# Attention heads scored and turned in groups on the tensor engine, in a two-layer streaming encoder

## The chip, the cores and the metric

The kernel runs on one core of a Trainium2 chip. Five engines of the core work side by side, each through its own list of instructions: TensorE (PE in the profile, with PEld for its loads of the stationary operand), VectorE (DVE), ScalarE (ACT), GpSimd (POOL) and SyncE (SP), which here only issues transfers. The metric is the device time of one execution in microseconds (us), lower is better.

## The reference

The input x is 256 tokens of 1024 numbers, in float32. Each of two layers is a SwiGLU feed-forward, a token mixing and a second feed-forward, each between two RMS norms:

```python
f = swiglu(rmsnorm(x, ffn1_pre_g[l]), ffn1_w_gate[l], ffn1_w_up[l], ffn1_w_down[l])
x = x + FFN_RESIDUAL_WEIGHT * rmsnorm(f, ffn1_post_g[l])
m = token_mixing(rmsnorm(x, mix_pre_g[l]), w_in[l], rel_bias[l], ..., w_out[l], lambda_init)
x = x + rmsnorm(m, mix_post_g[l])
f = swiglu(rmsnorm(x, ffn2_pre_g[l]), ffn2_w_gate[l], ffn2_w_up[l], ffn2_w_down[l])
x = x + FFN_RESIDUAL_WEIGHT * rmsnorm(f, ffn2_post_g[l])
```

The mixing projects x by w_in to queries, keys and values of 16 heads of 64 columns in three groups, and multiplies what they return by w_out:

- A, 6 heads: softmax attention over chunks of 64 tokens with a learned bias by distance.
- B, 4 heads: differential attention. A head has two softmax maps of 32 query and key columns each; the weights are `p[:, :, 0] - lam * p[:, :, 1]`, and the output goes through an RMS norm.
- C, 6 heads: stick-breaking attention, `a = jnp.where(strict, jnp.exp(log_beta + suffix), 0.0)` with a suffix sum of log-sigmoids.

## The kernel before

**The large products.** Tokens, weights and products are float32. A weight piece of mostly 512 KB comes by a transfer that SP issues, into one of four raw buffers. `Stream.ahead` splits it in two parts: ACT casts the high part (L142), DVE subtracts it for the low part (L143). A product of tokens and weights is then three matmuls (L376 to L378). These are called the main matmuls below.

**The mixing.** `mix` first computes the values. Then come 16 columns of queries and keys, `pp_0` to `pp_15`: 24 main matmuls each, of 128x256, into one PSUM bank. ACT copies each finished column to `qkT` (L842 or L844). Group B uses columns 0 to 3 (its heads 0 and 1 the columns 0 and 1, its heads 2 and 3 the columns 2 and 3), C columns 4 to 9, A columns 10 to 15. After these comes the product with w_out (`down`, main matmuls of 128x512 into `acc` banks).

**What sets the order.** The attention runs in the gaps of the main matmuls. `slot(n)` is called after every 6 main matmuls of the columns (so four times in a column; column f has slots 4f to 4f+3) and, from slot 64 on, after every 3 matmuls of the product with w_out. Each head or pair is a generator whose steps have due times in the table `PLAN`. All events are sorted by due time, and slot n issues those due before n+1. The program order on each engine follows from that; a consumer waits where its operand or its buffer is not ready. The pieces of splitting (`stream.ahead`) are also events, at n+0.9.

**The steps.** `head_b` has nine: scores of map 0, its softmax, scores of map 1, its softmax, `combine` (the difference of the maps, DVE), `turned` (three transposes on TensorE into a bank pT), `turned_copy` (ACT), the output, its scale. `pair_c` takes two heads: scores of each head in a step of its own, three passes of ACT, splitting, the suffix sums on TensorE (u1, u0), subtraction, the exponential, both outputs, the copy. `head_a` has scores, `soft`, the normalisation, `turned`, `turned_copy`, the output, and for odd heads the copy of the pair's output. In `soft`, DVE adds the bias and takes the row minimum (L723), and ACT takes the exponential (L725), in two blocks of 128 and 256 columns.

**Rows and columns of the array.** The scores of one B map contract over 32 partitions, at 64*(h%2)+32*m; those of an A or C head over 64, at 64*(h%2). The outputs of A and C heads go to 64 of the 128 output partitions (`columns_out`). The transposes and B's outputs use the full array.

**Banks.** PSUM has two tags of four banks each, `acc` and `rot`, and each tag hands out its banks in turn. `where(kind)` takes a kind's tag from the ranges in `PLAN["acc"]`. The columns pp are `rot`; the scores of B and C are `acc`; those of A are `acc` while the due time is below the end of the range `sA`.

Of the kernel before, what the change touches and what calls it, by code (L numbers as in the profile page):

```python
# [9 lines left out]
F32 = mybir.dt.float32  # L10
# [3 lines left out]
ALU = mybir.AluOpType  # L14
AX = mybir.AxisListType

P = 128
SEQ = 256
# [6 lines left out]
NH_A, NH_B, NH_C = 6, 4, 6  # L25
# [3 lines left out]
YA, YB, YC = 0, 384, 640  # L29
# [9 lines left out]
PLAN = {  # L39
    "qk": [  # L40
        7.05, 7.1, 14.05, 16.05, 19.05, 23.05, 27.05, 33.05, 35.05, 39.05, 43.05, 47.05, 53.05, 55.05,
        59.05, 63.05
    ],
# [5 lines left out]
    ],  # L49
# [4 lines left out]
    ],  # L54
    "a": [
        [49.1, 49.25, 51.05, 54.05, 57.05, 61.05],
        [50.05, 58.1, 58.92, 66.1, 68.1, 69.05, 72.05],
        [58.25, 58.3, 58.4, 62.05, 62.1, 67.05],
        [57.15, 58.35, 58.94, 63.1, 65.05, 69.1, 69.25],
        [68.05, 69.15, 70.05, 74.05, 76.05, 78.05],  # L60
        [65.1, 66.05, 66.25, 71.05, 71.1, 81.05, 83.05],
    ],
    "sub": [
        55.1, 64.05
# [11 lines left out]
    "gain": 81.1,  # L76
    "table": 82.05,
    "tail": 5,
    "acc": {"pT": [14, 26], "oB": [-10, 40], "oC": [-36, -14], "sA": [-140, 52]},
}  # L80
NSPLIT = 9

# [82 lines left out]
def trunk_kernel(  # L165
# [7 lines left out]
    nc = tc.nc  # L173
# [7 lines left out]
    small = ctx.enter_context(tc.tile_pool(name="small", bufs=3))  # L181
    psum = ctx.enter_context(tc.tile_pool(name="psum", bufs=4, space=bass.MemoryType.PSUM))
# [118 lines left out]
    def split_copy(hi, lo, src):  # L301
        nc.scalar.copy(hi, src)
        nc.vector.tensor_sub(lo, src, hi.bitcast(F32))
# [274 lines left out]
    def mix(i, l, turn1):  # L578
        lam_init = 0.8 - 0.6 * math.exp(-0.3 * l)
        v = act.tile([P, 2, D], F32, tag="bigl2", name=f"v{l}")  # L580
# [25 lines left out]
        c = stream.used  # L606
# [24 lines left out]
        qkT = act.tile([P, 16, SEQ], F32, tag="bigh1", name=f"qkT{l}")  # L631
# [3 lines left out]
        biasA = yb[:, 512:2048].rearrange("p (h s) -> p h s", h=NH_A)  # L635
# [81 lines left out]
        def soft(nm, s, bias, tag):  # L717


            p = work.tile([P, 512], F32, tag=tag, bufs=TA if tag == "ta" else 3, name=f"p_{nm}")[:, :384]  # L720
            st = small.tile([P, 4], F32, tag="st" + tag, name=f"st_{nm}")
            for t, (a, b) in enumerate(((0, P), (P, 384))):
                nc.vector.tensor_tensor_reduce(p[:, a:b], s[:, a:b], bias[:, SEQ - (b - a) : SEQ], 1.0, 3e38,  # L723
                                               ALU.add, ALU.min, accum_out=st[:, t : t + 1])
                nc.scalar.activation(p[:, a:b], p[:, a:b], AF.Exp, bias=st[:, t : t + 1], scale=-1.0,  # L725
                                     accum_out=st[:, 2 + t : 3 + t])
            return p, st

        def turned(nm, p):
            pT = psum.tile([P, 3, P], F32, tag=where("pT"), name=f"pT_{nm}")  # L730
            for j in range(3):
                nc.tensor.transpose(pT[:, j, :], p[:, j * P : j * P + P], ident)
            return pT

        def turned_copy(nm, pT):
            w = work.tile([P, 4, P], F32, tag="tc", bufs=3, name=f"wT_{nm}")[:, :3, :]
            nc.scalar.copy(w, pT)
            return w

        def columns_out(o, half, vh, w0, w1):  # L740
            oh = o[64 * half : 64 * half + 64, :]
            nc.tensor.matmul(oh, lhsT=vh[:, 0, :], rhs=w0, start=True, stop=False)
            nc.tensor.matmul(oh[:, P:], lhsT=vh[:, 1, :], rhs=w1, start=False, stop=True)

        def scores(nm, q, k, tag):
            s = psum.tile([P, 384], F32, tag=tag, name=f"s_{nm}")
            nc.tensor.matmul(s[:, 0:P], lhsT=q[:, 0:P], rhs=k[:, 0:P], start=True, stop=True)
            nc.tensor.matmul(s[:, P:384], lhsT=q[:, P:SEQ], rhs=k, start=True, stop=True)
            return s
# [35 lines left out]
        def subnorm():  # L785
            yb4 = yB.rearrange("p t (h d) -> p t h d", h=NH_B)
            sq = work.tile([P, 2, NH_B, 64], F32, tag="ta", bufs=TA, name=f"sq{l}")
            nc.vector.tensor_mul(sq, yb4, yb4)
            ss = small.tile([P, 2, NH_B], F32, tag="ssb", bufs=1, name=f"ssb{l}")
            nc.vector.tensor_reduce(ss, sq, AX.X, ALU.add)  # L790
            nc.vector.tensor_scalar(ss, ss, 1.0 / 64, EPS, ALU.mult, ALU.add)
            r = rstd_of(ss.rearrange("p t h -> p (t h)"), 2 * NH_B, f"sub{l}")
            yield
            for t in range(2):
                yv, sv = yb4[:, t], sq[:, t]
                rv = r[:, t * NH_B : (t + 1) * NH_B].unsqueeze(2).broadcast_to([P, NH_B, 64])
                nc.vector.tensor_mul(sv, yv, rv)
                nc.vector.tensor_mul(yv, sv, gsub.unsqueeze(1).broadcast_to([P, NH_B, 64]))
            yield

        pair_out = {}

        def head_a(h):

            nm = f"a{l}_{h}"
            fq, fk, b = 10 + 2 * (h // 2), 11 + 2 * (h // 2), 64 * (h % 2)
            s = scores(nm, qkT[b : b + 64, fq, :], qkT[b : b + 64, fk, :], where("sA"))
            yield
            p, st = soft(nm, s, biasA[:, h, :], "ta")
            yield  # L810
            ri = small.tile([P, 2], F32, tag="ri", bufs=6, name=f"ria{l}_{h}")
            nc.vector.reciprocal(ri, st[:, 2:4])
            for t, (a, c) in enumerate(((0, P), (P, 384))):
                nc.vector.tensor_scalar(p[:, a:c], p[:, a:c], ri[:, t : t + 1], None, ALU.mult)
            yield
            pT = turned(nm, p)
            yield
            w = turned_copy(nm, pT)
            yield
            if h % 2 == 0:  # L820
                pair_out[h // 2] = psum.tile([P, SEQ], F32, tag="rot", name=f"o_{nm}")
            vs = slice(YA + 64 * h, YA + 64 * h + 64)
            columns_out(pair_out[h // 2], h % 2, v[:, :, vs], w[:, 0:2, :], w[:, 2, :])
            yield
            if h % 2:
                keep_y(h // 2, pair_out[h // 2])
                yield

        def keep_y(k, src):
            split_copy(xT[:, k, 0], xT[:, k, 1], src.rearrange("p (t c) -> p t c", t=2))  # L830
# [17 lines left out]
        def where(kind):  # L848
            a, b = PLAN["acc"][kind]
            return "acc" if a <= now[0] < b else "rot"  # L850

        def at(x, do):
            events.append((x, len(events), do))

        def steps(slots, gen):
            for x in slots:
                at(x, lambda: next(gen))
# [4 lines left out]
            steps(PLAN["b"][h], head_b(h))  # L862
        for j in range(NH_C // 2):
            steps(PLAN["c"][j], pair_c(j))
        for h in range(NH_A):
            steps(PLAN["a"][h], head_a(h))
        steps(PLAN["sub"], subnorm())
        for k in range(2):
            steps(PLAN["turn"][k], turn_b(k))
# [60 lines left out]
    for i in range(3 * DEPTH):  # L930
        turn1 = mix(i, i // 3, turn1) if i % 3 == 1 else ffn(i, turn1)
# [36 lines left out]
```

## Time and profile before

| | |
|---|---|
| times of the runs | 1031.22, 1030.75, 1029.47 us (median 1030.75) |
| the profiled execution | 1030.83 us |
| its span in the profile | 1029.1 us, so 1.7 us lie outside it |
| mean granted TensorE clock | 0.994 of full speed |
| TensorE busy | 1011.4 us of the span |
| layer 0, columns pp to the start of `down` | about 227 to 312 us |

The second layer repeats the first 501.06 us later. In the lists below, a row of the timeline has the start in us from the start of the span, the duration in us, the engine, the line, the operation, the output and operands without their numbers, the shape, and a count where neighbours are taken together; behind it, in brackets, how long the engine stood idle before and for whom. For matmuls the end is modelled, so the starts are the firm numbers. In the view by stretches the columns are: stretch, its length, busy time of PE, PEld, DVE, ACT and POOL (with counts), granted TensorE clock, share of the DMA engines, GB/s.

### The profile page before, as it was taken

To read this page: it belongs to the slowest core of one execution; us is meant where nothing else is said; L and a number is where in the kernel's file an instruction comes from. 1 tells how busy PE (TensorE), PEld (TensorE's weight loads), DVE (VectorE), ACT (ScalarE), POOL (GpSimd) and SP (SyncE) were. 2 spreads that over 40 slices of the span, in tenths; PEclk is the share of its full clock that TensorE was granted. 3 is DMA by queue.
4 is the path that set the end of the run, shared out by engine and by line. 5 is a ranking of instruction groups with operands and counts; after the bars stand their busy time and mean duration, and the time that the engine had idled before them with its cause. 6 is when DMAs were issued, how large, how long until landed. Compare 5 with 4: busy or idle time off the path is not lost.

```text
span 1029.1 us, 16023 instructions
## 1 busy us (share of the span) xinstructions
PE 1011.4 (98%) x5940; PEld 881.9 (86%) x5940; DVE 673.2 (65%) x1345; ACT 588.1 (57%) x1265; POOL 43.2 (4%) x73
## 2 busy tenths in 40 slices
PE   8899999999999999999999999999999999999997
PEld 7788888898987988888899888888998789888886
DVE  5576774577775677665557767657678656866642
ACT  5475663466765556655445756545577645765531
POOL 4100000010000100000020000001001010000000
PEclk8999999999999999999999999999999999999999
DMA  8866656648344467656626765664944425865631
GB/s 261 234 200 185 188 180 229 185 149 228 106 124 123 136 201 221 200 189 218 209 86 203 247 198 172 227 198 117 255 135 128 124 98 158 252 196 185 217 119 41
DMA packets 151005, 183.16 MB, mean 178 GB/s; under 512 B 5744, under 2 KB 134896, under 8 KB 150928
## 3 DMA queue, kind: packets, MB, share of 16 engines
q1 hardware_dynamic: 148448, 174.08, 54.8%
q0 software_dynamic: 2192, 7.54, 2.5%
q8 instruction: 46, 0.75, 0.3%
q10 hardware_dynamic: 288, 0.52, 0.1%
q14 instruction: 31, 0.25, 0.1%
HBM read 181.08 MB, written 1.05 MB: 177 GB/s over the span
## 4 chain that ended last, share of the span: by engine, by line
PE 89%; DMA 3%; ACT 3%; DVE 3%; POOL 1%; issue 1%; SPq 0%; POOLq 0%; DVEq 0%; ACTq 0%
PE pg L408 13%; PE pu L408 13%; PE acc L376 9%; PE acc L378 9%; PE acc L377 9%; PE pg L410 7%; PE pu L410 7%; PE pp L376 3%; PE pp L377 2%; PE pp L378 2%; DMA raw<-in_ffn_w_gate_dram 2%; DVE wlo L143 1%; PE pu L377 1%; PE pu L378 1%; PE pu L376 1%; PE pg L376 1%
## 5 line engine op out<-in xcount | busy, mean ns | idle before, releaser
L143 DVE TENSOR_TENSOR wlo<-raw,whi 128x512 fp32r<-128x512 f32 (+1 forms) x625 | 395.9, 689 | 159.3 <-ACT whi L142 158.8
L142 ACT CAST whi<-raw 128x512 fp32r<-128x512 f32 x630 | 349.9, 617 | 121.3 <-PE acc L378 69.3
L408 PE MATMUL pg<-xT,whi 128*128 128x512 f32 x576 | 206.9, 401 | 0.0
L408 PE MATMUL pu<-xT,whi 128*128 128x512 f32 x576 | 205.2, 399 | 0.0
L410 PE MATMUL pg<-xT,wlo 128*128 128x256 f32 x576 | 162.2, 282 | 0.0
L410 PE MATMUL pu<-xT,wlo 128*128 128x256 f32 x576 | 161.8, 281 | 0.0
L376 PE MATMUL acc<-whi,hh 128*128 128x512 f32 x352 | 137.3, 390 | 0.0
L378 PE MATMUL acc<-whi,hl 128*128 128x512 f32 x352 | 137.0, 389 | 0.0
L377 PE MATMUL acc<-wlo,hh 128*128 128x512 f32 x352 | 137.0, 389 | 0.0
L408 PEld LDWEIGHTS pg<-xT,whi 128*128 128x128 f32 x576 | 108.8, 189 | 26.8
L408 PEld LDWEIGHTS pu<-xT,whi 128*128 128x128 f32 x576 | 108.2, 188 | 27.1
L410 PEld LDWEIGHTS pg<-xT,wlo 128*128 128x128 f32 x576 | 109.4, 190 | 0.0
L410 PEld LDWEIGHTS pu<-xT,wlo 128*128 128x128 f32 x576 | 108.8, 189 | 0.0
L378 PEld LDWEIGHTS acc<-whi,hl 128*128 128x128 f32 x352 | 66.1, 188 | 13.7
L376 PEld LDWEIGHTS acc<-whi,hh 128*128 128x128 f32 x352 | 66.1, 188 | 13.7
L377 PEld LDWEIGHTS acc<-wlo,hh 128*128 128x128 f32 x352 | 66.1, 188 | 13.5
L376 PE MATMUL pp<-xT,whi 128*128 128x256 f32 x256 | 76.2, 298 | 0.0
L377 PE MATMUL pp<-xT,whi 128*128 128x256 f32 x256 | 72.3, 282 | 0.0
L378 PE MATMUL pp<-xT,wlo 128*128 128x256 f32 x256 | 72.3, 282 | 0.0
L376 PEld LDWEIGHTS pp<-xT,whi 128*128 128x128 f32 x256 | 48.8, 191 | 7.3 <-issue 6.3
L415 ACT COPY side_pu<-pu 128x256 f32<-128x256 f32 x72 | 26.0, 368 | 49.4 <-PE pu L410 49.4
L416 DVE TENSOR_TENSOR h<-pu,side_pu 128x256 f32<-128x256 f32 x72 | 29.8, 422 | 29.6 <-ACT side_pu L415 29.4
(247 smaller groups left out, 1485.1 us busy)
## 6 DMA issues: line engine op xcount, KB each, us to landing
raw<-in_ffn_w_gate_dram SPq DMA_DIRECT2D x88, 512.0 KB, 4.7
raw<-in_ffn_w_up_dram SPq DMA_DIRECT2D x88, 512.0 KB, 4.6
raw<-in_ffn_w_down_dram SPq DMA_DIRECT2D x88, 512.0 KB, 4.3
raw<-in_w_in_dram SPq DMA_DIRECT2D x36, 512.0 KB, 5.4
raw<-in_w_out_dram SPq DMA_DIRECT2D x16, 512.0 KB, 3.5
raw<-in_w_in_dram SPq DMA_DIRECT2D x8, 576.0 KB, 4.2
gpost<-in_ffn_post_g_dram POOLq DMA_DIRECT2D x4, 512.0 KB, 4.2
raw<-in_w_in_dram SPq DMA_DIRECT2D x4, 384.0 KB, 3.6
```

The lines of the kernel that those rows point to most:

```text
L142: self.nc.scalar.copy(self.hi[:, a:b], raw[:, a:b])
L143: (lo or self.nc.vector).tensor_sub(self.lo[:, a:b], raw[:, a:b], self.hi.bitcast(F32)[:, a:b])
L376: nc.tensor.matmul(ps, lhsT=ah, rhs=bh, start=first, stop=False)
L377: nc.tensor.matmul(ps, lhsT=ah, rhs=bl, start=False, stop=False)
L378: nc.tensor.matmul(ps, lhsT=al, rhs=bh, start=False, stop=last)
L408: nc.tensor.matmul(ps.rearrange("p a t -> p (a t)"), lhsT=wh[:, k % 4, cs], rhs=xT[:, k].rearrange("p a t c -> p (a t c)"), start=k == 0, ...
L410: nc.tensor.matmul(ps[:, 1, :], lhsT=wl[:, k % 4, cs], rhs=xT[:, k, 0].rearrange("p t c -> p (t c)"), start=False, stop=k == KT - 1)
L415: nc.scalar.copy(side, ps[:, 1, :])
L416: nc.vector.tensor_add(out[:, j, :], ps[:, 0, :], side)
```

## The change

The table of due times and the A heads' generator change; no instruction is added or removed, and no transfer moves.

- B: the four maps of heads 0 and 1 are all scored in slot 15 (before, one in slot 14 and three in slot 15), those of heads 2 and 3 all in slot 22 (before, two in slot 22 and two in slot 25).
- C: the two heads of the first pair are scored one directly behind the other in slot 28 (before, both in slot 27, with other events between), those of the last pair in slot 43 (before, slots 42 and 43).
- A: heads go by pairs. Each step issues both heads' instructions: scores in slots 49, 57 and 65, transposes in 55, 64 and 72, outputs in 60, 68 and 77. Before, each head had slots of its own, except the transposes and copies.
- The range in which A's scores take `acc` banks ends at 58 instead of 52.

Line numbers behind the table are 3 lower than before.

```diff
@@ PLAN
     "b": [
-        [14.1, 15.1, 15.2, 15.3, 15.4, 26.1, 26.25, 30.05, 33.2],
+        [15.02, 15.1, 15.2, 15.3, 15.4, 26.1, 26.25, 30.05, 33.2],
         [15.05, 15.15, 15.25, 15.35, 15.45, 25.05, 26.05, 33.1, 33.15],
         [22.05, 22.1, 22.15, 22.2, 22.25, 26.15, 26.2, 30.94, 31.05],
-        [25.1, 25.15, 25.2, 25.25, 25.3, 30.1, 32.05, 44.05, 44.1],
+        [22.07, 22.12, 22.17, 22.22, 22.27, 30.1, 32.05, 44.05, 44.1],
     ],
     "c": [
-        [27.1, 27.92, 27.94, 30.92, 32.1, 39.1, 39.15, 39.2, 42.05, 44.15],
-        [39.25, 39.3, 40.05, 40.1, 44.2, 49.05, 49.15, 49.2, 53.1, 57.1],
-        [42.1, 43.1, 45.05, 45.1, 48.05, 58.05, 58.15, 58.2, 62.15, 62.2],
+        [28.1, 28.15, 28.2, 30.92, 32.1, 39.1, 39.15, 39.2, 42.05, 44.15],
+        [39.25, 39.3, 40.05, 40.1, 44.2, 49.05, 49.15, 49.2, 53.1, 56.05],
+        [43.1, 43.15, 45.05, 45.1, 48.05, 58.05, 58.15, 58.2, 62.15, 62.2],
     ],
     "a": [
-        [49.1, 49.25, 51.05, 54.05, 57.05, 61.05],
-        [50.05, 58.1, 58.92, 66.1, 68.1, 69.05, 72.05],
-        [58.25, 58.3, 58.4, 62.05, 62.1, 67.05],
-        [57.15, 58.35, 58.94, 63.1, 65.05, 69.1, 69.25],
-        [68.05, 69.15, 70.05, 74.05, 76.05, 78.05],
-        [65.1, 66.05, 66.25, 71.05, 71.1, 81.05, 83.05],
+        [49.1, 49.25, 51.05, 55.05, 57.05, 60.05, 62.05],
+        [57.15, 58.35, 59.1, 64.1, 65.05, 68.05, 69.25],
+        [65.1, 66.05, 67.05, 72.05, 72.1, 77.05, 78.05],
     ],
...
-    "acc": {"pT": [14, 26], "oB": [-10, 40], "oC": [-36, -14], "sA": [-140, 52]},
+    "acc": {"pT": [14, 26], "oB": [-10, 40], "oC": [-36, -14], "sA": [-140, 58]},
@@ mix
-        def head_a(h):
...
+        def pair_a(j):
+            fq, fk = 10 + 2 * j, 11 + 2 * j
+            nms = [f"a{l}_{2 * j + m}" for m in range(2)]
+            ss = [
+                scores(nms[m], qkT[64 * m : 64 * m + 64, fq, :], qkT[64 * m : 64 * m + 64, fk, :], where("sA"))
+                for m in range(2)
+            ]
+            yield
+            ps = [soft(nms[m], ss[m], biasA[:, 2 * j + m, :], "ta") for m in range(2)]
+            yield
...
+            yield
+            pTs = [turned(nms[m], ps[m][0]) for m in range(2)]
+            yield
+            ws = [turned_copy(nms[m], pTs[m]) for m in range(2)]
+            yield
+            o = psum.tile([P, SEQ], F32, tag="rot", name=f"o_{nms[0]}")
+            for m in range(2):
+                vs = slice(YA + 64 * (2 * j + m), YA + 64 * (2 * j + m) + 64)
+                columns_out(o, m, v[:, :, vs], ws[m][:, 0:2, :], ws[m][:, 2, :])
+            yield
+            keep_y(j, o)
+            yield
...
-        for h in range(NH_A):
-            steps(PLAN["a"][h], head_a(h))
+        for j in range(NH_A // 2):
+            steps(PLAN["a"][j], pair_a(j))
```

**First place: TensorE, slots 14 and 15.** The names are: `pp_3` and `pp_4` are columns, `s_b_0_0` the scores of B, head 0, map 0. The number behind a name is that of the tile. Before:

```order
L378 MATMUL pp_3_2486<-xT,wlo_2252 128x256
L747 MATMUL s_b_0_0_2514<-qkT_2377 128x128
L748 MATMUL s_b_0_0_2514<-qkT_2377 128x256
L376 MATMUL pp_3_2486<-xT,whi_2251 128x256
L377 MATMUL pp_3_2486<-xT,whi_2251 128x256
L378 MATMUL pp_3_2486<-xT,wlo_2252 128x256
...
L747 MATMUL s_b_1_0_2523<-qkT_2377 128x128
L748 MATMUL s_b_1_0_2523<-qkT_2377 128x256
L747 MATMUL s_b_0_1_2538<-qkT_2377 128x128
```

And now:

```order
L375 MATMUL pp_3_2486<-xT,wlo_2252 128x256
L744 MATMUL s_b_0_0_2520<-qkT_2377 128x128
L745 MATMUL s_b_0_0_2520<-qkT_2377 128x256
L744 MATMUL s_b_1_0_2523<-qkT_2377 128x128
L745 MATMUL s_b_1_0_2523<-qkT_2377 128x256
L744 MATMUL s_b_0_1_2538<-qkT_2377 128x128
L745 MATMUL s_b_0_1_2538<-qkT_2377 128x256
L744 MATMUL s_b_1_1_2541<-qkT_2377 128x128
L745 MATMUL s_b_1_1_2541<-qkT_2377 128x256
L373 MATMUL pp_4_2578<-xT,whi_2285 128x256
```

The lone map moved behind the end of column pp_3, to the other three. Slot 22, for heads 2 and 3, takes the same shape.

**Second place: ACT, softmaxes of B heads 2 and 3.** `p_b_2_0` are the weights of head 2, map 0; `wT_b_1` is the turned copy of head 1. Before:

```order
L725 ACTIVATE p_b_2_0_2635,st_b_2_0_2636<-p_b_2_0_2635,st_b_2_0_2636 128x128
L725 ACTIVATE p_b_2_0_2635,st_b_2_0_2636<-p_b_2_0_2635,st_b_2_0_2636 128x256
L725 ACTIVATE p_b_2_1_2644,st_b_2_1_2645<-p_b_2_1_2644,st_b_2_1_2645 128x128
L725 ACTIVATE p_b_2_1_2644,st_b_2_1_2645<-p_b_2_1_2644,st_b_2_1_2645 128x256
L844 COPY qkT_2377<-pp_5_2613 128x256
L142 CAST whi_2664<-raw_2465 128x512 x2
L725 ACTIVATE p_b_3_0_2692,st_b_3_0_2693<-p_b_3_0_2692,st_b_3_0_2693 128x128
L725 ACTIVATE p_b_3_0_2692,st_b_3_0_2693<-p_b_3_0_2692,st_b_3_0_2693 128x256
```

And now:

```order
L722 ACTIVATE p_b_2_0_2638,st_b_2_0_2639<-p_b_2_0_2638,st_b_2_0_2639 128x128
L722 ACTIVATE p_b_2_0_2638,st_b_2_0_2639<-p_b_2_0_2638,st_b_2_0_2639 128x256
L722 ACTIVATE p_b_3_0_2644,st_b_3_0_2645<-p_b_3_0_2644,st_b_3_0_2645 128x128
L722 ACTIVATE p_b_3_0_2644,st_b_3_0_2645<-p_b_3_0_2644,st_b_3_0_2645 128x256
L722 ACTIVATE p_b_2_1_2656,st_b_2_1_2657<-p_b_2_1_2656,st_b_2_1_2657 128x128
L722 ACTIVATE p_b_2_1_2656,st_b_2_1_2657<-p_b_2_1_2656,st_b_2_1_2657 128x256
L722 ACTIVATE p_b_3_1_2662,st_b_3_1_2663<-p_b_3_1_2662,st_b_3_1_2663 128x128
L722 ACTIVATE p_b_3_1_2662,st_b_3_1_2663<-p_b_3_1_2662,st_b_3_1_2663 128x256
L843 COPY qkT_2377<-pp_5_2613 128x256
L139 CAST whi_2689<-raw_2465 128x512 x2
```

Head 3's exponentials moved ahead of the copy of column pp_5 and of a pair of casts, and stand between the two maps of head 2.

**Third place: ACT and TensorE around columns pp_13 and pp_14 (slots 49 to 56).** `e_c_1` is the exponential of the second C pair, `p_a_0` the weights of A head 0, `pT_a_0` its turned weights in PSUM. ACT before:

```order
L703 ACTIVATE e_c_1_2901<-z_c_1_2900 128x768
L725 ACTIVATE p_a_0_3064,st_a_0_3065<-p_a_0_3064,st_a_0_3065 128x128
L725 ACTIVATE p_a_0_3064,st_a_0_3065<-p_a_0_3064,st_a_0_3065 128x256
L142 CAST whi_3089<-raw_2861 128x512 x2
L842 ACTIVATE qkT_2377<-pp_12_3030 128x256
L844 COPY qkT_2377<-pp_13_3097 128x256
```

ACT now:

```order
L700 ACTIVATE e_c_1_2901<-z_c_1_2900 128x768
L722 ACTIVATE p_a_0_3067,st_a_0_3068<-p_a_0_3067,st_a_0_3068 128x128
L722 ACTIVATE p_a_0_3067,st_a_0_3068<-p_a_0_3067,st_a_0_3068 128x256
L722 ACTIVATE p_a_1_3073,st_a_1_3074<-p_a_1_3073,st_a_1_3074 128x128
L722 ACTIVATE p_a_1_3073,st_a_1_3074<-p_a_1_3073,st_a_1_3074 128x256
L139 CAST whi_3099<-raw_2861 128x512 x2
L841 ACTIVATE qkT_2377<-pp_12_3030 128x256
L843 COPY qkT_2377<-pp_13_3107 128x256
```

TensorE now, at the end of pp_13:

```order
L375 MATMUL pp_13_3107<-xT,wlo_2606 128x256
L729 MATMUL pT_a_0_3139<-ident,p_a_0_3067 128x128 x3
L729 MATMUL pT_a_1_3143<-ident,p_a_1_3073 128x128 x3
L373 MATMUL pp_14_3154<-xT,whi_2689 128x256
L374 MATMUL pp_14_3154<-xT,whi_2689 128x256
```

The copies of pp_12 and pp_13 moved behind the exponentials of a second A head, and a pair of transposes stands at the end of pp_13, where before one head's stood six main matmuls earlier.

More of the change, by code (lines that the diff above doesn't have):

```diff
@@ L799, in subnorm @@
             yield
-        pair_out = {}
-        def head_a(h):
-            nm = f"a{l}_{h}"
-            fq, fk, b = 10 + 2 * (h // 2), 11 + 2 * (h // 2), 64 * (h % 2)
-            s = scores(nm, qkT[b : b + 64, fq, :], qkT[b : b + 64, fk, :], where("sA"))
+        def pair_a(j):
[5 more added lines that the diff above has]
+            ]
             yield
-            p, st = soft(nm, s, biasA[:, h, :], "ta")
+            ps = [soft(nms[m], ss[m], biasA[:, 2 * j + m, :], "ta") for m in range(2)]
             yield
[L811 to L814, printed above, removed]
+            for m, (p, st) in enumerate(ps):
+                ri = small.tile([P, 2], F32, tag="ri", bufs=6, name=f"ri{nms[m]}")
+                nc.vector.reciprocal(ri, st[:, 2:4])
+                for t, (a, c) in enumerate(((0, P), (P, 384))):
+                    nc.vector.tensor_scalar(p[:, a:c], p[:, a:c], ri[:, t : t + 1], None, ALU.mult)
             yield
-            pT = turned(nm, p)
+            pTs = [turned(nms[m], ps[m][0]) for m in range(2)]
             yield
-            w = turned_copy(nm, pT)
+            ws = [turned_copy(nms[m], pTs[m]) for m in range(2)]
             yield
[L820 to L823, printed above, removed]
+            o = psum.tile([P, SEQ], F32, tag="rot", name=f"o_{nms[0]}")
+            for m in range(2):
+                vs = slice(YA + 64 * (2 * j + m), YA + 64 * (2 * j + m) + 64)
+                columns_out(o, m, v[:, :, vs], ws[m][:, 0:2, :], ws[m][:, 2, :])
             yield
-            if h % 2:
-                keep_y(h // 2, pair_out[h // 2])
-                yield
+            keep_y(j, o)
+            yield
         def keep_y(k, src):
```

## The prediction

> **What bounds the kernel now.** I read the page first: its busy times and the engines' shares of the chain of waits.
>
> ```profile
> span 1029.1 us, 16023 instructions
> PE 1011.4 (98%) x5940; PEld 881.9 (86%) x5940; DVE 673.2 (65%) x1345; ACT 588.1 (57%) x1265; POOL 43.2 (4%) x73
> PE 89%; DMA 3%; ACT 3%; DVE 3%; POOL 1%; issue 1%; SPq 0%; POOLq 0%; DVEq 0%; ACTq 0%
> ```
>
> TensorE is busy for 98% of the span and carries 89% of the chain. To see whether that holds in the stage of the change, I read the view by stretches for the columns of layer 0, and beside it the two stretches in which the clock fell.
>
> ```profile
> 227.00:330.00 103.00, 102.57 (x712) 87.89 (x711) 74.51 (x215) 67.22 (x167) 3.84 (x6) 1.00 0.53 159
> 8.00:17.00 9.00, 7.03 (x32) 6.20 (x32) 5.72 (x8) 6.22 (x14) 4.57 (x5) 0.62 0.98 327
> 43.00:47.00 4.00, 3.18 (x12) 2.78 (x13) 4.00 (x10) 2.29 (x5) 0.00 (x0) 0.57 0.85 250
> ```
>
> In the stage TensorE is busy for 102.57 of 103 us at full clock; DVE (74.51) and ACT (67.22) have room, though in lumps. So TensorE time removed here shortens the span, unless a tile it needs isn't ready yet when it comes earlier. Both questions need single rows.
>
> **What a visit costs.** I call it a visit when TensorE leaves the main matmuls for small tiles and returns. The timeline of TensorE, slots 14, 15 and 22:
>
> ```profile
> 242.57 0.28 PE L377 MATMUL pp<-xT,whi 128*128 128x256 f32 x1
> 242.69 0.28 PE L378 MATMUL pp<-xT,wlo 128*128 128x256 f32 x1
> 242.90 0.48 PE L747 MATMUL s_b<-qkT 32*128 32x128 f32 x2
> 243.74 0.39 PE L376 MATMUL pp<-xT,whi 128*128 128x256 f32 x1
> 243.97 0.28 PE L377 MATMUL pp<-xT,whi 128*128 128x256 f32 x1
> ...
> 244.65 0.51 PE L747 MATMUL s_b<-qkT 32*128 32x128 f32 x6
> 245.52 0.39 PE L376 MATMUL pp<-xT,whi 128*128 128x256 f32 x1
> ...
> 251.24 0.50 PE L747 MATMUL s_b<-qkT 32*128 32x128 f32 x4 [0.42 <-ACT qkT L844]
> 252.10 0.39 PE L376 MATMUL pp<-xT,whi 128*128 128x256 f32 x1
> ```
>
> Main matmuls start every 0.12 us (242.57 to 242.69). The visit with one map takes 242.69 to 243.97, which is 1.28 where two spacings would be 0.24: it costs 1.04. Of that 0.84 is its length (242.90 to 243.74) and 0.20 lies at its two seams. Three maps side by side are 0.87 long, two 0.86. A further map on other rows is thus nearly free; the visit is what costs. The same for groups C and A:
>
> ```profile
> 258.31 0.70 PE L667 MATMUL s_c<-qkT 64*128 64x256 f32 x2
> 258.99 0.70 PE L667 MATMUL s_c<-qkT 64*128 64x256 f32 x2
> 259.84 0.39 PE L376 MATMUL pp<-xT,whi 128*128 128x256 f32 x1
> ...
> 271.87 0.71 PE L667 MATMUL s_c<-qkT 64*128 64x256 f32 x4
> 272.73 0.39 PE L376 MATMUL pp<-xT,whi 128*128 128x256 f32 x1
> ...
> 286.35 0.48 PE L747 MATMUL s_a<-qkT 64*128 64x128 f32 x2
> 287.20 0.39 PE L376 MATMUL pp<-xT,whi 128*128 128x256 f32 x1
> ...
> 289.54 0.66 PE L742 MATMUL o_c<-e_c,v 128*64 128x256 f32 x4
> 290.34 0.39 PE L376 MATMUL pp<-xT,whi 128*128 128x256 f32 x1
> ...
> 299.61 0.65 PE L742 MATMUL o_a<-wT_a,v 128*64 128x256 f32 x2
> 300.40 0.39 PE L376 MATMUL pp<-xT,whi 128*128 128x256 f32 x1
> ```
>
> The first C pair runs one head after the other (second 0.68 later; 1.53 in all), the second pair side by side in 0.86. One A score takes 0.85. One A output takes 0.79, and the two outputs of a C pair, which go to different columns of the array, together 0.80.
>
> **What the change saves, per layer.**
>
> - B: visits of 1.04, 1.07, 1.06 and 1.06 become two of four maps, 0.89 + 0.20 = 1.09 each (by the step from two to three): 4.23 - 2.18 = 2.05.
> - C: first pair 1.53 - 0.86 = 0.67. In the last pair the first head already stands behind another tile in one visit, so only a length goes: 0.84. Together 1.51.
> - A scores: six visits become three. No pair of A scores side by side is in the trace; the C pair on the same rows is the nearest row. 3 x 1.04 = 3.12; at the other end, a second head 0.68 later as in the first C pair, it would be 3 x 0.36 = 1.1.
> - A outputs: four alone (0.99 with seams) and two directly behind each other on the same columns (0.68 + 0.99 = 1.67) cost 5.63; three pairs, priced by the C pair's outputs, 3 x 1.00. Saves 2.63, at the other end 3 x 0.68 less: 0.6.
> - Transposes use the whole array, and their number is the same: nothing. DVE, ACT and the transfers do the same work: nothing by themselves.
>
> Sum 9.31 us. [...]
>
> **What is given back.** Work that TensorE saves ahead of a tile that another engine makes is lost there. I carried the new order along the rows of ACT and DVE; four places come out.
>
> ```profile
> 250.82 0.36 ACT L844 COPY qkT<-pp 128x256 f32<-128x256 f32 x1
> ...
> 254.07 0.41 ACT L725 ACTIVATE p_b<-p_b,st_b 128x128 f32<-128x128 f32 x1 [1.58 <-DVE st_b L723]
> ...
> 254.97 0.39 ACT L725 ACTIVATE p_b<-p_b,st_b 128x128 f32<-128x128 f32 x1
> ...
> 255.84 0.35 ACT L844 COPY qkT<-pp 128x256 f32<-128x256 f32 x1
> ...
> 287.66 0.85 ACT L703 ACTIVATE e_c<-z_c 128x768 f32<-128x768 f32 x1 [2.07 <-DVE z_c L701]
> 288.41 0.39 ACT L725 ACTIVATE p_a<-p_a,st_a 128x128 f32<-128x128 f32 x1
> ...
> 290.31 0.37 ACT L842 ACTIVATE qkT<-pp 128x256 f32<-128x256 f32 x1
> ```
>
> *First, slot 22.* The scores of heads 2 and 3 need ACT's copy of column pp_3, which ends at 250.82 + 0.36 = 251.18; TensorE already waited for it until 251.24. ACT gets there through the softmaxes of heads 0 and 1 and a pair of casts, none of which starts earlier for the slot-14 visit that is gone. So the 1.04 saved there turns into wait: 1.0 given back. Behind it TensorE has pp_5's matmuls, which then run as before.
>
> *Second, slot 26.* The rows of TensorE and DVE:
>
> ```profile
> 256.45 1.22 PE L732 MATMUL pT_b<-ident,p_b 128*128 128x128 f32 x6
> ...
> 256.43 0.75 DVE L768 SCALAR_TENSOR_TENSOR p_b<-p_b,fac,p_b 128x128 f32<-128x128 f32 x2
> 257.10 1.29 DVE L143 TENSOR_TENSOR wlo<-raw,whi 128x512 fp32r<-128x512 f32 x2
> ```
>
> The six transposes are those of heads 0 and 2. Head 2's combine on DVE ends at 257.18, and its transposes follow at once: no slack. In the new order ACT does head 3's first map between head 2's two maps. One map takes 0.90 there (254.07 to 254.97), so the combine ends 0.90 later, while TensorE, with the slot-25 visit gone, comes 1.06 earlier: 1.96 given back. Late next on ACT are the copy of pp_5 and the pair of casts behind head 3's exponentials, 1.8 later than at 255.84; the copy is needed from slot 28 on, where TensorE is then as late as before. DVE's subtraction behind the combine is late by 0.9 too.
>
> *Third, slot 53.* The outputs of the second C pair need e_c, ready at 287.66 + 0.85 = 288.51; TensorE came at 289.54, so 1.03 were spare. It would come some 1.7 earlier there (9.31 up to that point less the two waits), so 0.6 at most is lost; the chain ahead of e_c itself starts earlier by 0.3 or so. I take 0.3, bounds 0 and 0.6.
>
> *Fourth, slots 55 and 56.* With two transposes side by side the rot banks go pp_12, pp_13, o_c_1, pT_a_0, pT_a_1, pp_14: the second transpose takes pp_12's bank and pp_14 takes pp_13's, so both wait for ACT's copies. These now stand behind the exponentials of a second A head, another 0.9 by the map just priced; the transposes cover some of it. I take 0.35, bounds 0.2 and 0.7.
>
> Elsewhere each operand is ready with room. Per layer 9.31 - 1.0 - 1.96 - 0.65 = 5.7; two layers 11.4. The profiled execution took 1030.83 with its span of 1029.1, practically the median of 1030.75: **1019.4 us**.
>
> **The rivals.** They need the longest waits of TensorE in this trace:
>
> ```profile
> PE pt L371 <- DVE xg_pre L348: 3.4, 2, 2.8
> PE pth L510 <- DVE ht L504: 3.1, 1, 3.1
> PE pth L510 <- ACT sgt L497: 1.3, 1, 1.3
> ```
>
> (us in total, times, longest.) After the 3.1 us wait the clock fell as at 43 to 47, mean 0.57. After 1.3 it did not. The new waits, some 1.5 and 2, lie between.
>
> - *The clock falls once per layer*, at the second wait. A fall costs (1 - 0.57) x 4 = 1.7: 1019.4 + 3.4 = 1022.8. For it speaks that two waits lie within 6 us; against it that the matmuls between keep TensorE busy. [...] Chance 0.10.
> - *The A pairs don't overlap*, so the change does not do there what it says: 3 x 0.68 x 2 for the outputs alone gives 1023.5, for scores too 1027.6. [...] Chance 0.05.
> - *ACT and DVE set the pace*: every saving comes back as a wait, 1030.8. They are busy for 65 to 72% of the stage. [...] But from slot 28 on most tiles have over 1 us spare. Chance 0.05.
> - *Slower: the clock falls at both waits in both layers and stays low*, as at 8 to 17 us, where it was 0.62 over 9 us: (1 - 0.62) x 9 = 3.4 per fall, four falls 13.7, 1033.1. It decides from 11.4/4 = 2.85 per fall. Against it: that stretch was starved by transfers (0.98 of the DMA engines). Chance 0.06.
>
> **How the numbers follow.** The forecast has 0.74. Its own ends: the third and fourth place nil (-1.3), the second 0.5 smaller per layer (-1.0) and a few hundredths off each visit (-0.6) give 1016.5; both at their upper bounds (+1.3) and in each layer one pair of subtractions (1.29) late for TensorE (+2.6) give 1023.3. With the first rival and part of the second the range is 1016.5 to 1024.5. What a measurement of this kernel can tell from no change is about 0.2%, 2 us. Faster by more: forecast, first and second rival, 0.89 less 0.03 for tails, 0.86; the third rival and those tails are no difference, 0.08; slower 0.06.
>
> **What would show it.** In the changed kernel's timeline: groups of eight s_b, 0.89 long; the first C pair 0.86; o_a in fours at 0.80. Among TensorE's waits, per layer: s_b on ACT's copy of the column, some 1.5; pT_b on DVE's p_b, some 2; small ones at o_c and pp. TensorE's busy time falls by about 18 us, its span by 11. The clock stays 1.00 from 240 to 265. Wrong would be: a long wait at another tile, a clock under 1.00 there, or pairs that start 0.7 apart.

## The result, and the profile after

The changed kernel takes 1021.36 us (median of 4 runs, 1017.56 to 1022.65), the kernel before 1030.37 (4 runs). The ratio is 0.9907, with a 95% interval of 0.9878 to 0.9935: faster, as forecast, inside the range, and 2 us slower than the forecast of 1019.4. The profiled execution took 1022.65 us. Its page has these lines in place of those shown of before:

```profile
span 1020.7 us, 16031 instructions
PE 996.7 (98%) x5940; PEld 874.6 (86%) x5940; DVE 672.3 (66%) x1345; ACT 586.4 (57%) x1265; POOL 43.2 (4%) x73
PE 83%; DVE 5%; DMA 5%; ACT 4%; issue 1%; POOL 0%; SPq 0%; DVEq 0%; POOLq 0%; ACTq 0%
```

TensorE's busy time fell by 14.7 us and the span by 8.4. In the chain, TensorE's share went from 89 to 83%, and those of DVE, the transfers and ACT rose by 2, 2 and 1 points: some of what TensorE gave up is now waiting. The view of TensorE's waits (us in total, times, longest) names three that were not there, or hardly (the one at s_b was 0.4, once):

```profile
PE pT_b L729 <- ACT p_b L722: 3.6, 2, 1.8
PE s_b L744 <- ACT qkT L843: 2.6, 2, 1.4
PE pT_a L729 <- ACT qkT L841: 0.5, 2, 0.2
```

The small tiles themselves overlap as the prediction had it (`...` marks rows left out). From the timeline of TensorE, each group with the main matmul behind it:

```profile
243.10 0.52 PE L744 MATMUL s_b<-qkT 32*128 32x128 f32 x8
243.99 0.39 PE L373 MATMUL pp<-xT,whi 128*128 128x256 f32 x1
...
293.81 0.50 PE L744 MATMUL s_a<-qkT 64*128 64x128 f32 x4
294.67 0.38 PE L373 MATMUL pp<-xT,whi 128*128 128x256 f32 x1
...
297.94 0.66 PE L739 MATMUL o_a<-wT_a,v 128*64 128x256 f32 x4
298.75 0.39 PE L373 MATMUL pp<-xT,whi 128*128 128x256 f32 x1
```

Four B maps take 0.89 us, two A scores 0.86, two A outputs 0.81.

And the clock fell. The timeline behind head 2's transposes, and the view by stretches around it:

```profile
257.05 0.74 PE L729 MATMUL pT_b<-ident,p_b 128*128 128x128 f32 x3 [1.78 <-ACT p_b L722]
257.55 0.36 PE L373 MATMUL pp<-xT,whi 128*128 128x256 f32 x1
...
258.62 0.41 PE L373 MATMUL pp<-xT,whi 128*128 128x256 f32 x1
258.83 0.41 PE L374 MATMUL pp<-xT,whi 128*128 128x256 f32 x1
```

```profile
254.50:257.80 3.30, 1.51 (x12) 1.11 (x11) 2.44 (x15) 3.30 (x15) 0.00 (x0) 1.00 0.56 196
257.90:261.30 3.40, 3.40 (x20) 3.02 (x18) 2.90 (x6) 2.77 (x7) 0.00 (x0) 0.51 0.16 36
261.40:264.80 3.40, 3.40 (x32) 3.27 (x29) 1.22 (x5) 1.92 (x3) 0.00 (x0) 1.00 0.72 253
```

From 257.9 to 261.3 main matmuls start every 0.21 us, not every 0.12, and the granted clock is 0.51. Layer 1 shows the same from 756.3 on.

**How the time of a stage was compared.** All kernels here issue the same 5376 main matmuls in the same order. I subtracted the start of each in one execution from that of the same one before. Between the mixing stages this difference stays constant to 0.2 us. Ahead of the first mixing stage it differs from one execution to the next by up to 4 us (-3.1 to +1.1) in kernels that are the same there. That can account for most of the spread of a kernel's runs, which reached 7 us, and it is why the times of the variants below, nearly all between 1016 and 1023, can hardly be told apart. The mixing stage alone is compared instead: below, its gain is the change of that difference from the columns' start to the end of the product with w_out, split at slot 55 (negative: earlier than before). It comes from one profiled execution of each kernel.

| us | layer 0: to slot 55 | behind it | sum | layer 1: to slot 55 | behind it | sum |
|---|---|---|---|---|---|---|
| the change | +0.53 | -4.92 | -4.39 | +1.35 | -4.92 | -3.57 |
| the change, a second profile | +0.20 | -4.92 | -4.72 | +0.48 | -4.92 | -4.44 |
| B alone | +0.31 | 0.00 | +0.31 | +0.16 | 0.00 | +0.16 |
| A and C | -0.59 | -4.92 | -5.51 | +0.53 | -4.92 | -4.39 |
| A alone | -0.33 | -4.93 | -5.26 | -0.08 | -4.93 | -5.01 |
| seq | +0.80 | -4.91 | -4.11 | +0.37 | -4.93 | -4.56 |
| seq_late | +0.49 | -4.92 | -4.43 | +1.55 | -4.92 | -3.37 |
| pack | +0.11 | -4.92 | -4.81 | +0.54 | -4.91 | -4.37 |
| pack_late | -0.65 | -4.93 | -5.58 | -0.20 | -4.92 | -5.12 |
| pack_spread | -1.70 | -3.57 | -5.27 | -1.82 | -3.57 | -5.39 |
| pack_qk3 | -2.51 | -3.57 | -6.08 | -1.18 | -3.57 | -4.75 |
| pack_pool | -0.74 | -4.93 | -5.67 | -0.43 | -4.92 | -5.35 |
| pool_spread | -2.91 | -4.28 | -7.19 | -2.33 | -4.28 | -6.61 |

Two profiles of the same kernel, the first two rows, differ by 0.3 and 0.9 us in the sums, all of it ahead of slot 55: smaller differences between rows tell nothing. In pack_spread, pack_qk3 and pool_spread the first A transposes come behind slot 55, which moves some 0.65 us from the first column of a layer to the second; there only the sums compare.

The first row is the reading of the result. By slot 55 of each layer the changed kernel has saved nothing: it is even 0.5 to 1.4 us late. All of its gain lies behind slot 55, where the A pairs' scores and outputs are, and there it is the same to 0.01 us in every kernel that has these pairs at these slots.

### The profile page after: what moved, and what is told of

It reads as the page before. It is cut to its first block, busy times and chain, and to the rows that moved or that the text cites. A ratio compares the mean times of both kernels' runs of the same rounds, so it can differ in the third digit from the quotient of the medians.

```text
span 1020.7 us, 16031 instructions
## 1 busy us (share of the span) xinstructions
PE 996.7 (98%) x5940; PEld 874.6 (86%) x5940; DVE 672.3 (66%) x1345; ACT 586.4 (57%) x1265; POOL 43.2 (4%) x73
## 4 chain that ended last, share of the span: by engine, by line
PE 83%; DVE 5%; DMA 5%; ACT 4%; issue 1%; POOL 0%; SPq 0%; DVEq 0%; POOLq 0%; ACTq 0%
PE pg L405 13%; PE pu L405 13%; PE acc L373 9%; PE acc L375 9%; PE acc L374 9%; PE pg L407 7%; PE pu L407 7%; DVE wlo L140 3%; DMA raw<-in_w_in_dram 2%; PE pp L373 2%; DMA raw<-in_ffn_w_up_dram 2%; PE pp L375 2%; PE pp L374 1%; ACT p_b L722 1%; PE pu L374 1%
```

## The experiments

Two theories stood at the start. The first: head 3's exponentials between the two maps of head 2 cost the wait at pT_b, and that wait the clock; B is the faulty part. The second: B is sound and A and C lose through banks and the order on ACT.

**B alone, and A and C alone.** The table rows of B and of A and C, each taken over alone:

```diff
 b_only: the kernel before with
-        [14.1, 15.1, 15.2, 15.3, 15.4, 26.1, 26.25, 30.05, 33.2],
+        [15.02, 15.1, 15.2, 15.3, 15.4, 26.1, 26.25, 30.05, 33.2],
-        [25.1, 25.15, 25.2, 25.25, 25.3, 30.1, 32.05, 44.05, 44.1],
+        [22.07, 22.12, 22.17, 22.22, 22.27, 30.1, 32.05, 44.05, 44.1],
 ac_only: the changed kernel with these two rows as before
```

> Only the B part of the change (four maps in slot 15, four in slot 22); A and C as before. Theory 1 (head 3's softmax between the maps of head 2 makes TensorE wait at head 2's transposes, and that wait makes the clock fall): per layer -0.93 and -0.92 for the two visits, +0.8 for the wait at s_b, +1.8 for the wait at pT_b, +1.4 for the slow clock, together +2.2, so some 1034.8 us, clock 0.991. Theory 2 (the B part is sound and the shortfall comes from A and C, through banks and the order on ACT): -0.5 to -1.0 per layer, 1028.4 to 1029.4, clock 0.994.

Measured: 1031.99 us (10 runs), ratio 1.0023 (1.0005 to 1.0040); in the mixing +0.31 and +0.16. The B part alone saves nothing, which goes against the second theory. But it costs less than the first one expected. The waits are there, 3.5 us at pT_b in all; in the profiled execution the clock stayed up:

```profile
252.00:255.60 3.60, 1.83 (x16) 1.51 (x14) 2.81 (x19) 3.60 (x18) 0.00 (x0) 1.00 0.67 261
255.60:259.00 3.40, 3.39 (x27) 2.92 (x28) 3.33 (x11) 3.40 (x9) 0.00 (x0) 1.00 0.02 7
```

The first stretch holds the wait of 1.77, which ended at 255.54; the second is at full clock. The same wait (1.78) in the whole change was followed by a slow stretch. So the length of the wait alone does not decide. This execution took 1028.96 us, the fastest of the ten; four of the others, of 1031.80 to 1034.31 us, show a mean clock of 0.991 where none of the kernel before beside them is under 0.992. Whether the clock fell in their mixing is not shown, since they left no trace.

There is a second reason for the small loss. The first C pair runs side by side here, with C's rows as before:

```profile
256.93 0.71 PE L667 MATMUL s_c<-qkT 64*128 64x256 f32 x4
```

That gives back 0.66 us per layer between slots 26 and 29, about what the sum had put down to C (0.67). In the kernel before, the second head started at 258.99 and 760.05, each 0.06 us after DVE's read of head 3's first scores; so it probably waited for their bank, and not for the first head.

> Only the A and C parts of the change; B as before. Theory 1: per layer 0.67 + 0.84 for C, 3.1 + 2.6 for A, less 0.65 at o_c and the second transpose: -6.5, so 1017.4 us and faster than the whole change, clock 0.994, no wait at pT_b. Theory 2: no better than the whole change, 1021 to 1024, with the waits inside the A steps.

Measured: 1020.81 us, ratio 0.9908 (0.9873 to 0.9943); in the mixing -5.51 and -4.39, no slow stretch and no wait at pT_b. On average that is 1.0 per layer better than the whole change in its first profile, but 1.6 per layer short of -6.5. The rest went where I had said each operand was ready with room. Ahead of slot 55 TensorE lost 0.4 us at the outputs of heads 0 and 2 (slot 30), 0.2 and 0.65 at the suffix sums of C (slots 39 and 49), and at the second C pair's outputs:

```profile
287.61 0.66 PE L739 MATMUL o_c<-e_c,v 128*64 128x256 f32 x4 [0.76 <-ACT e_c L700]
```

Neither theory holds as put: both parts lose what they save ahead of slot 55, each at the next tile that ACT or DVE makes.

**Head 2's wait.** In seq the two heads' softmaxes run one head after the other; in seq_late head 2's transposes stand in slot 28 as well.

```diff
-        [22.07, 22.12, 22.17, 22.22, 22.27, 30.1, 32.05, 44.05, 44.1],
+        [22.3, 22.35, 22.4, 22.45, 22.5, 30.1, 32.05, 44.05, 44.1],
 seq_late, besides:
-        [22.05, 22.1, 22.15, 22.2, 22.25, 26.15, 26.2, 30.94, 31.05],
+        [22.05, 22.1, 22.15, 22.2, 22.25, 28.05, 28.07, 30.94, 31.05],
```

> The whole change, but the softmaxes of heads 2 and 3 one head after the other (the four maps still scored side by side in slot 22). Theory 1: the wait at pT_b falls from 1.78 to 0.9, the clock stays up: 0.9 + 1.4 per layer less than the whole change, 1016.8 us. Rival (the clock falls at a wait of 0.9 too, or because of the wait at s_b before it): only the 0.9 per layer comes back, 1019.6, clock 0.991.

> As the run before, and head 2's transposes (with their copy) stand in slot 28 instead of slot 26. Theory 1: no wait at pT_b is left: another 0.9 per layer, 1015.0 us. Rival (the stall only moves on, to the output o_b of head 2 or to the scores s_c): as the run before, 1016.8, with the wait at that tile.

Measured: seq 1022.68 us, ratio 0.9918 (0.9885 to 0.9950); seq_late 1022.58, ratio 0.9914 (0.9884 to 0.9943). Both expectations failed. In seq the wait at pT_b is 0.9 in layer 1 and none in layer 0, where the clock fell behind a wait of 1.90 at s_b. But a new wait is there, at the next column, and ACT's timeline of seq, below the row of TensorE, shows why:

```profile
260.31 0.39 PE L373 MATMUL pp<-xT,whi 128*128 128x256 f32 x1 [1.20 <-ACT qkT L843]
```

```profile
259.41 0.49 ACT L722 ACTIVATE p_b<-p_b,st_b 128x256 f32<-128x256 f32 x1
259.81 0.18 ACT L722 ACTIVATION_READ_ACCUMULATOR p_b<-p_b,st_b 128x1 f32 x1
259.91 0.35 ACT L843 COPY qkT<-pp 128x256 f32<-128x256 f32 x1
```

The next column takes a bank that ACT empties only when it has copied pp_5, and that copy stands behind all of head 3's exponentials. In seq_late the late transposes take that bank, and wait 2.2 us for the same copy.

**The maps side by side, ACT and DVE as before.** In pack the generator issues both maps' scores before both softmaxes, so that head 3 can be scored in slot 22 and still have its softmax in slot 25, behind the copy of pp_5. The diff shows the rows of heads 2 and 3; those of heads 0 and 1 follow the new order of steps in the same way.

```diff
-            ps = []
+            ps, ss = [], []
             for m in range(2):
                 b = 64 * (h % 2) + 32 * m
-                s = scores(f"b{l}_{h}_{m}", ...)
+                ss.append(scores(f"b{l}_{h}_{m}", ...))
                 yield
-                ps.append(soft(f"b{l}_{h}_{m}", s, alibi[:, h, :], ("ta", "tb")[m]))
+            for m in range(2):
+                ps.append(soft(f"b{l}_{h}_{m}", ss[m], alibi[:, h, :], ("ta", "tb")[m]))
                 yield
...
-        [22.05, 22.1, 22.15, 22.2, 22.25, 26.15, 26.2, 30.94, 31.05],
-        [22.07, 22.12, 22.17, 22.22, 22.27, 30.1, 32.05, 44.05, 44.1],
+        [22.05, 22.07, 22.1, 22.2, 22.25, 26.15, 26.2, 30.94, 31.05],
+        [22.06, 22.08, 25.15, 25.25, 25.3, 30.1, 32.05, 44.05, 44.1],
 pack_late:   head 2's transposes and copy at 28.05, 28.07 (26.15, 26.2)
 pack_spread: besides, outputs of the second C pair at 54.1 (53.1), first A transposes at 56.1 (55.05)
 pack_qk3:    besides, the copy of pp_3 at 15.01 (16.05)
```

> The whole change, but heads 2 and 3 of B keep the order of the kernel before on ACT and DVE: their four maps are scored side by side in slot 22, and head 3's softmax is issued in slot 25 again, behind the copy of column pp_5 and a pair of casts. Theory (head 3's exponentials ahead of that copy are what B's second group costs, as waits at pT_b and at the column's bank, and as a slow clock): a wait of some 1.1 us at pT_b, none at pp, clock up in the mixing; the mixing gains 5.4 us in layer 0 and 4.5 in layer 1 against the kernel before, as with A and C alone; about 1020.4 us. Rival (four maps side by side are the cause, whatever stands behind them): a wait of 1.8 at pT_b and slow stretches, 4.0 per layer.

> As the run before, and head 2's transposes and their copy stand in slot 28 instead of 26. Theory: the wait of 1.1 at pT_b is gone; one more us per layer, part of which (0.4) comes back at o_c of the second C pair, so 6.0 and 5.1 per layer, 1019.2 us. Rival (the wait moves on in full): o_c waits 1.1 longer than in the run before, 5.4 and 4.5.

> As the run before, and the outputs of the second C pair stand in slot 54 (not 53), the first pair of A transposes in slot 56 (not 55). Theory: the waits at o_c (0.2 to 1.2) and at the second transpose (0.24) go: 7.2 and 6.3 per layer, 1016.8 us. Rival (later tiles now wait, a o_a or pp_15's bank): nothing gained on the run before.

> As the run before, and ACT's copy of column pp_3 is issued ahead of the softmaxes of heads 0 and 1 (15.01, not 16.05). Theory: the wait at s_b in slot 22 (0.8 to 1.9) is gone: 8.0 and 7.1 per layer, 1015.2 us. Rival (the softmaxes of heads 2 and 3 are bound by DVE, which is no earlier): the wait moves to pT_b, nothing gained.

Measured: pack 1021.96 us, ratio 0.9909 (0.9887 to 0.9932); in the mixing -4.81 and -4.37, no slow stretch, no wait at the column, 0.9 at pT_b. Between slots 25 and 29 it lost 0.2 and 0.4 us in the two layers, where the change lost 2.6 and 2.8 in its first profile. So at that place head 3's exponentials ahead of the copy are what cost more than the visit saves; the four maps side by side are not. Over the whole stage little of it is kept: the second profile of the change has -4.72 and -4.44. Like A and C, pack loses 0.4 at slot 30, 0.65 at slot 49 and 0.8 at slot 53. pack_late: 1019.18, ratio 0.9886 (0.9869 to 0.9902), -5.58 and -5.12. The wait at pT_b is gone. Over A and C this is 0.1 and 0.7 per layer, no more than two profiles of one kernel differ by; a gain of B's part is not shown. pack_spread: 0.9884 (0.9869 to 0.9899), -5.27 and -5.39, nothing more that can be told. pack_qk3: 0.9885 (0.9871 to 0.9900), -6.08 and -4.75. In the last two the rival held each time: the waits at o_c and s_b went, and TensorE waits 0.56 at A's first transposes (for ACT's copy of a column) and 0.8 and 1.5 at pT_b (for DVE).

**A alone, the change once more, and relief for DVE.** By now a new theory stood: ahead of slot 55, ACT and DVE make the tiles no earlier, whatever TensorE saves. A alone is the changed kernel with B's and C's rows as before. In pack_pool nine weight subtractions per layer go to GpSimd:

```diff
-                at(n + 0.9, lambda k=k: stream.ahead(k))
+                at(n + 0.9, lambda k=k, n=n: stream.ahead(k, nc.gpsimd if n in (15, 19, 28, 33, 35, 41, 47) else None))
```

> Only the A part of the change; B and C as before. Theory 4 (what is saved ahead of slot 55 is given back there, since ACT and DVE make the tiles no earlier; only A's savings behind slot 55 stay): the mixing gains 4.9 us behind slot 55 and 0 to 0.5 ahead of it in each layer, 4.9 to 5.4, nearly as much as with A and C; about 1020.5 us. Rival (C's part counts in full): 1.5 per layer less than with A and C, so 4.0 and 2.9.

> The whole change once more, unaltered, for one more profile. [...] Rival (the wait alone decides): the same two falls as in the first profile.

> As the run with head 2's transposes in slot 28 (pack_late), and 9 weight subtractions per layer of slots 15 to 41 are done by GpSimd instead of DVE (9 times 0.69 us less on DVE, 9 times 1.35 on GpSimd). Theory 4 (DVE and ACT set the pace ahead of slot 55): some of the 4.5 us that B, C and the first A pair save there now stays, 6.5 to 8 per layer against 5.6 and 5.1. Rival (ACT alone sets it, or GpSimd and DVE slow each other): 5.6 and 5.1 or less.

Measured: A alone 1019.27 us, ratio 0.9880 (0.9856 to 0.9903), -5.26 and -5.01 in the mixing: as this theory expected. A's pairs by themselves gain as much as A and C (-5.51, -4.39) or the whole change, and no wait of 1 us is left in the mixing.

The change once more took 1019.13 us. Its waits and its slow stretches are not those of the first profile:

```profile
PE s_b L744 <- ACT qkT L843: 2.9, 2, 2.4
PE pT_b L729 <- ACT p_b L722: 2.2, 2, 1.8
```

```profile
247.00:250.00 3.00, 0.61 (x16) 0.56 (x16) 2.66 (x10) 3.00 (x11) 0.00 (x0) 1.00 0.27 79
250.50:253.80 3.30, 3.30 (x17) 3.30 (x17) 3.30 (x18) 1.72 (x8) 0.00 (x0) 0.50 0.49 173
```

In layer 0 the clock fell behind a wait of 2.4 at s_b, and TensorE was then so late that at pT_b it waited only 0.39; in layer 1 it fell behind 1.78 at pT_b. A wait of 1.78 at pT_b thus came in layer 1 alone. Why ACT's copy of pp_3 came 0.5 us late in one layer of this execution and 2.4 in the other I did not settle.

pack_pool: 1019.71 us, ratio 0.9892 (0.9868 to 0.9916), -5.67 and -5.35, against -5.58 and -5.12 without it: hardly anything. DVE's groups between 240 and 291 us, first of pack_late, then of pack_pool, and GpSimd's there (busy us, mean ns):

```profile
L140 DVE TENSOR_TENSOR wlo<-raw,whi 128x512 fp32r<-128x512 f32 x24 | 15.6, 684 | 0.8 <-ACT whi L139 0.7
L685 DVE TENSOR_TENSOR l_c<-yb,h_c 128x512 fp32r<-128x512 f32 x2 | 1.4, 682 | 0.0
```

```profile
L140 DVE TENSOR_TENSOR wlo<-raw,whi 128x512 fp32r<-128x512 f32 x15 | 10.6, 727 | 0.5 <-ACT whi L139 0.5
L685 DVE TENSOR_TENSOR l_c<-yb,h_c 128x512 fp32r<-128x512 f32 x2 | 2.5, 1232 | 0.0
L140 POOL TENSOR_TENSOR wlo<-raw,whi 128x512 fp32r<-128x512 f32 x9 | 12.5, 1412 | 26.3 <-ACT whi L139 26.3
```

DVE has nine subtractions less, 5.0 us, but some of its other operations take longer here (the combines of B's maps took 0.58 and 0.74 us on average, not 0.35 and 0.48; one l_c took 1.78, not 0.68, and the two subtractions of GpSimd beside it 3.43 together, others 1.3 each), so that its busy time in the stretch falls only from 41.7 to 41.0. So this run does not answer whether a DVE that is really relieved would help.

**The two put together.** pool_spread is pack_pool with the second C pair's outputs at 54.1 and A's first transposes at 57.02 (55.05):

> As the run with nine subtractions on GpSimd (pack_pool), with the outputs of the second C pair in slot 54 (not 53) and the first pair of A transposes in slot 57 (not 55), so that both come when their tiles are ready. Theory (the waits of 1.11 and 0.23 there are the last that cost): they go, 6.5 and 6.2 per layer in the mixing, about 1017.5 us. Rival (ACT's chain is late by as much at the next tile): 5.7 and 5.4 as before, 1019.

Measured: 1016.57 us (6 runs; before 1029.91), ratio 0.9882 (0.9860 to 0.9905); in the mixing -7.19 and -6.61, the best of all, and somewhat more than expected. The rows of TensorE's timeline at the two places:

```profile
286.12 0.66 PE L739 MATMUL o_c<-e_c,v 128*64 128x256 f32 x4 [0.38 <-ACT e_c L700]
...
289.19 0.87 PE L729 MATMUL pT_a<-ident,p_a 128*128 128x128 f32 x6
```

The wait at o_c has gone from 1.11 to 0.38, that at the transposes to nothing. At slot 55 this kernel is 2.9 and 2.3 us ahead. By its mixing stage it is faster than the kernel before and than the change; by the times alone its ratio can't be told from those of A alone or pack_late, whose intervals overlap with it.

## Why the prediction came out as it did

**What TensorE saves was right.** The visits removed measured 0.94 (slot 14) and 0.92 (slot 25) for B, and slot 15 came 0.08 better: 1.94, where the sum had 2.05; 0.85 for the last C pair (0.84 in the sum). Behind slot 55 the sum, by its own prices, has two of the three A scores (2.08) and the outputs (2.63), together 4.71; with the 0.33 of one head's transposes, which now lie ahead of slot 55, it is 5.04, measured 4.92. The A outputs, on all rows and different columns, took 0.81 for two, where one alone took 0.79. The other end of the sum, a second head 0.68 later, was read from the first C pair, where B alone shows that it was probably a wait.

**The first two waits were right in place, and on average in size.** At slot 22 TensorE gave back 0.80 and 1.47 in the two layers (1.0 in the sum), and 2.00 and 0.60 in the second profile; at slot 26, 1.76 and 1.92 (1.96 in the sum): head 3's exponentials between head 2's maps, each 0.88, as in the order shown. In layer 0 of the second profile, where TensorE was already late, slot 26 took 0.37. The first wait was for ACT's copy of a column; the second was for exponentials that read and write p_b, as ACT's rows of seq show.

**The step that failed was the clock**, by its chance and not by its price. Between slots 26 and 29 TensorE lost 0.87 and 0.86 where the first C pair should have saved 0.67: 1.53 per layer, where the rival had 1.7. The forecast left it out: the waits of 1.5 and 2 lay between one that did (3.1) and one that did not (1.3), and it argued that the matmuls between the two waits keep TensorE busy. It gave the falls 0.10. The clock fell in both layers of both profiles, and a clock under 1.00 between 240 and 265 us was one of the prediction's own signs of being wrong. With two falls the rival's time was 1022.8, and the profiled execution took 1022.65; that the two agree so well is luck, since the second profile, with two falls as well, took 1019.13.

**The third and fourth place were right in size.** 0.18 at o_c and some 0.3 around the second transpose, together some 0.5 against 0.65 in the sum. The working of the third place names 9.31 as saved up to there; by the prediction's own terms it is 4.60 (B, C and one pair of A scores), and that less the two waits gives the 1.6 to 1.7 it went on with.

**"Elsewhere each operand is ready with room" was right only because TensorE came late.** With B's losses taken away (A and C), TensorE met the tiles of slots 30, 39, 49 and 53 too early and lost some 2.0 us there. So the third rival, that ACT and DVE set the pace, is right for one part of the stage: ahead of slot 55, where no kernel got more than 0.75 us ahead without moving the transposes behind it. pool_spread got 2.9 and 2.3 us ahead, some 0.65 of it by that move. The prediction had looked at the busy shares of the whole stage, 72 and 65%. That a chain of single tiles can set the pace at such shares was in its own timeline rows, but it was followed at four places only.

**The sum.** Against 11.4 us for both layers the two profiles show 7.96 and 9.16 in the mixing. In the first the two slow stretches (1.53 each) make up 3.1 of the 3.4 that are missing; in the second, layer 0 lost more at s_b and less at pT_b. The median of the runs, 2 us above the forecast, carries the spread ahead of the mixing besides.

## What to carry to other kernels

Small matmuls on other rows or columns were nearly free beside each other here (0.89 us for four maps, 0.84 for one; 0.81 for two A outputs, 0.79 for one); what costs is the visit. But a visit that is dropped pays only where the next tile from another engine has time to spare: follow each consumer to its producer's end, in the new order on that engine, before counting it. And where a change takes a lot from several places, ask in which the gain would stay if the others were left as they are: here A's pairs alone do it all, and B's cost as much as they saved. Putting the softmaxes back behind the copy that TensorE waits for took the clock's falls away, but no clear gain came of it before the later tiles were moved as well.

## What the runs showed of the hardware

**The clock fell behind some waits and not behind others.** In the first profile of the change slow stretches began at 42.9 (the start of the kernel), 257.9 and 756.3 us, in the second profile those of the mixing at 250.5 and 752.2; each lasted some 3.4, at a granted clock of 0.50 or 0.51. Waits of TensorE, and the clock behind them:

| kernel, layer | wait, us | clock |
|---|---|---|
| the change, 0 and 1 | 1.78, 1.78 | fell, fell |
| the change, second profile | 2.39, 1.78 | fell, fell |
| seq, 0 | 1.90 | fell |
| seq_late, 0 and 1 | 2.19, 2.19 | fell, fell |
| pack_spread, 0 | 1.63 | stayed |
| B alone, 0 and 1 | 1.77, 1.77 | stayed, stayed |
| the change, second profile, ahead of layer 0's mixing | 2.67 | stayed |

```profile
249.46 0.53 PE L744 MATMUL s_b<-qkT 32*128 32x128 f32 x8 [1.63 <-ACT qkT L844]
```

In the mixing this row of pack_spread and the waits of 1.77 in B alone are those of the table without a fall, while each of 1.78 was followed by one. The last row goes further: in the second profile of the change that wait ended at 44.15, and the clock stayed up behind it:

```profile
42.30:45.65 3.35, 1.50 (x9) 1.36 (x10) 3.35 (x8) 3.29 (x8) 0.00 (x0) 1.00 0.75 222
45.70:49.10 3.40, 3.40 (x22) 2.98 (x21) 2.56 (x6) 0.65 (x2) 0.00 (x0) 1.00 0.77 242
```

So the length of a wait does not decide by itself; what else counts is not shown. A wait of 1.8 cost 1.5 us more in the change and nothing more in B alone.

**GpSimd and DVE slowed each other in pack_pool.** An l_c subtraction on DVE beside GpSimd's took 1.78 us, where others took 0.68; GpSimd's two beside it took 3.43 together, where others took 1.3 each.
